# Gated linear attention: the product of keys and values in three rounded parts

## The chip, the cores and the metric

The kernel runs on one core of one Trainium2 chip. The metric is the device time of one execution in microseconds (us), as the median of several runs. A core has five engines that run side by side, each with a queue worked off in order: TensorE (PE in the profile, its weight loads PEld), VectorE (DVE), ScalarE (ACT), GpSimd (POOL) and SyncE (SP), which here only issues DMA transfers. Matrix products write to the banks of PSUM, and the other operands live in SBUF.

## The reference

One layer of a decoder: a normalised input is projected into the operands of two groups of heads, differential softmax attention (8 heads) and gated linear attention (4 heads). Both results are normalised and gated, joined, and projected out. The sequence has 1024 positions. Of this the change touches the gated heads alone:

```python
def gla_chunked(q, k, v, log_a):
    """S_t = diag(exp(log_a_t)) S_{t-1} + k_t^T v_t ; o_t = q_t S_t (q scaled by dk^-0.5)."""
    ...
    attn = jnp.where(causal, jnp.einsum('bhnik,bhnjk->bhnij', q_dec, k_inv), 0.0)
    o_intra = jnp.einsum('bhnij,bhnjv->bhniv', attn, v)

    def step(state, xs):
        qd, kt, vc, dl = xs
        o = jnp.einsum('bhck,bhkv->bhcv', qd, state)
        state = state * dl[..., None] + jnp.einsum('bhck,bhcv->bhkv', kt, vc)
        return state, o
```

The state of a head is 128 x 256 float32. The second product in `step`, keys times values, is what is changed.

## The kernel before, in words

The program has three stages. The first normalises the input and multiplies it by the input weights, in blocks of a seven-product scheme (`order`, `step`, `go`); the second is the softmax attention together with half of the output projection; the third ends the output projection. The gated heads have no stage of their own: they are a generator, `gla(g)`, put into the list `fill`, and each step of the first stage, twelve products of 512 columns in a bank x, y or z, advances it to its next `yield` (steps of the value blocks advance it twice). So work of the gated heads stands between the steps of the projection. TensorE's instructions keep the order in which the program writes them (`mm` and `tr` pin it); the instructions of the other engines and the DMA issues are put in order by the planner of the framework, and then run in that order on each engine's queue.

A projection step needs weights split into a rounded high part and a low part: a cast `w` on ScalarE, then a subtraction on VectorE, made up to three steps ahead in a ring of five. A product of full precision is then three rounded (fp32r) products, high by high, low by high and high by low. The gated heads, before, multiply in full float32 instead.

`gla(g)` works through a head in two halves of 512 positions, four blocks of 128 each. A half goes like this, with the number of steps in between:

- `gla_loads` has brought keys and queries (`kq`), values (`gv`) and decayed queries (`gqd`) from DRAM. The tile of the gates (`gg`) is taken.
- One step later: `pa`, the four blocks of scores, copied to `a`, the first half of the tile `gan`, and masked there by GpSimd; `pk`, the four keys transposed, copied to `kn`, the second half of `gan`. SP issues the load of the gates.
- Three steps later (two in the last half of all): `kv`, keys times values of a block into half a bank, and `gu`, the state, updated from it on VectorE. A head needs seven updates, four in its first half and three in its second.
- Two steps later: `gpo`, the output of each block from `a` and the state, copied to `go`.
- One step later: the loads of the next half are asked for, and the squares are summed (`sqs`, `sq_hl`).
- Three steps later (two in the last half): `gms`, the sum over the head, and the norm: `r` on ScalarE, then on VectorE and ScalarE `go` scaled, multiplied by the gates, and split again. The high part is written over the gates in `gg`, the low part over `go`, and SP stores both to `mixe` in DRAM.
- One step later the next half begins.

All of these tiles live in the pool `kp`, where each tag has one buffer: `q0` holds `kq`, `k0` holds `gv`, `ks0` holds `go`, `ks1` holds `gg`, and `k1` holds `gan`, then `sqs` and `sq_hl`. Who takes a tag next has to wait until all work on the tile before, transfers too, is done; the framework adds these waits.

Of the kernel before, what the change touches and what calls it, by code (L numbers as in the profile page):

```python
# [8 lines left out]
F32 = mybir.dt.float32  # L9
F32R = mybir.dt.float32r  # L10
AF = mybir.ActivationFunctionType
ALU = mybir.AluOpType
PSUM = bass.MemoryType.PSUM

P = 128
# [16 lines left out]
def hymba_kernel(  # L32
# [21 lines left out]
    pe, sp = nc.tensor, nc.sync  # L54
# [20 lines left out]
    act, dve, pool = Queue(nc.scalar), Queue(nc.vector), Queue(nc.gpsimd)  # L75

    def fp(t):
        return t.bitcast(F32)

    def cols(half):  # L80
        return slice(half * 512, half * 512 + 512)
# [40 lines left out]
    gg_d = [tc.dram_tile([2, P, S], F32, name=f"gg{g}_d") for g in range(GLA_HEADS)]  # L122
# [14 lines left out]
    def take_bank(shape, name):  # L137
        i = free.pop(0)
        return bank(i, shape, name), i
# [3 lines left out]
    def mm(*a, **k):  # L143
        tc.keep_in_program_order(pe.matmul(*a, **k))  # L144

    def tr(dst, src):
        tc.keep_in_program_order(pe.transpose(dst, src, ident))  # L147
# [29 lines left out]
    kp = ctx.enter_context(tc.tile_pool(name="kp", bufs=1))  # L177
# [6 lines left out]
    def t_c(name, dt=F32):  # L184
        return t2k("c", 4, name, dt)
# [838 lines left out]
    def gla_loads(g, half):  # L1024

        if g < GLA_HEADS and (g, half) not in loaded:
            cs = cols(half)
            kq = kp.tile([P, 2, 512], F32, tag="q0", name="kq")
            v = kp.tile([P, 2, 4, P], F32, tag="k0", name="gv")
            if not spare:  # L1030
                spare.append(kp.tile([P, 2, 512], F32, tag="q1", name="gqd"))
            qd = spare[0][:, 0]
            sp.dma_start(kq[:, 0], gq_d[g][2, :, cs])
            sp.dma_start(kq[:, 1], gq_d[g][0, :, cs])
            for t in range(2):
                sp.dma_start(v[:, t], gv_d[g][t, :, half * 4 : half * 4 + 4, :])
            sp.dma_start(qd, gq_d[g][1, :, cs])
            loaded[g, half] = kq, v, qd
        return loaded.get((g, half))

    def gla(g):

        u = None
        for half in range(2):
            cs = cols(half)
            kq, v, qd = gla_loads(g, half)
            gates = kp.tile([P, 2, 512], F32, tag="ks1", name="gg")
            yield
            if not g and not half:
                yield  # L1050
                yield
            o = kp.tile([P, 2, 512], F32, tag="ks0", name="go")
            an = kp.tile([P, 2, 4, P], F32, tag="k1", name="gan")
            a, kn = an[:, 0], an[:, 1]
            pa, ib = take_bank([P, 4, P], "pa")
            for i in range(4):
                c = slice(i * P, i * P + P)
                mm(pa[:, i, :], kq[:, 0, c], kq[:, 1, c], start=True, stop=True)
            free.append(ib)
            act.copy(a, pa)  # L1060
            pool.affine_select(
                a, a, [[0, 4], [1, P]], ALU.is_ge, 0.0, base=0, channel_multiplier=-1
            )
            pk, ib = take_bank([P, 4, P], "pk")
            for i in range(4):
                tr(pk[:, i, :], kq[:, 0, i * P : i * P + P])
            free.append(ib)
            act.copy(kn, pk)
            for t in range(2):
                sp.dma_start(gates[:, t], gg_d[g][t, :, cs])  # L1070
            last = g == GLA_HEADS - 1 and half == 1
            for _ in range(2 if last else 3):
                yield
            us = [u]
            for m in range(2):
                kv, ib = take_bank([P, 2, 256], "kv")
                n = half * 4 + 2 * m
                for i in range(min(2, NT - 1 - n)):
                    mm(
                        kv[:, i].rearrange("p (t c) -> p t c", c=P), kn[:, 2 * m + i, :],  # L1080
                        v[:, :, 2 * m + i, :], start=True, stop=True,
                    )
                for i in range(min(2, NT - 1 - n)):
                    u1, u = u, ap.tile([P, 256], F32, tag="gu", name="gu", bufs=5)
                    if u1 is None:
                        dve.tensor_copy(u, kv[:, i])
                    else:
                        dve.scalar_tensor_tensor(
                            u, u1, dsteps[g][:, n + i : n + i + 1], kv[:, i], ALU.mult, ALU.add
                        )  # L1090
                    us.append(u)
                free.append(ib)
            yield
            yield
            for m in range(2):
                po, ib = take_bank([P, 2, 256], "gpo")
                for i in range(2):
                    c = slice((2 * m + i) * P, (2 * m + i + 1) * P)
                    for t in range(2):
                        oc = po[:, t, i * P : (i + 1) * P]  # L1100
                        mm(
                            oc, v[:, t, 2 * m + i, :], a[:, 2 * m + i, :],
                            start=True, stop=(us[2 * m + i] is None),
                        )
                        if us[2 * m + i] is not None:
                            u_t = us[2 * m + i][:, t * P : (t + 1) * P]
                            mm(oc, u_t, qd[:, c], start=False, stop=True)
                act.copy(o[:, :, m * 256 : m * 256 + 256], po)
                free.append(ib)
            yield  # L1110
            gla_loads(*((g, 1) if half == 0 else (g + 1, 0)))

            sqs = kp.tile([P, 2, 512], F32, tag="k1", name="sqs")
            for t in range(2):
                act.activation(sqs[:, t], o[:, t], AF.Square)
            sq = t_c("sq")
            dve.tensor_tensor(sq, sqs[:, 0], sqs[:, 1], ALU.add)
            act.copy(sqs[:64, 1], sq[64:])
            dve.tensor_tensor(sq[:64], sq[:64], sqs[:64, 1], ALU.add)
            hl = kp.tile([P, 2, 512], F32R, tag="k1", name="sq_hl")[:, 0]  # L1120
            act.copy(hl[:64], sq[:64])
            dve.tensor_tensor(hl[64:], sq[:64], fp(hl[:64]), ALU.subtract)
            for _ in range(2 if last else 3):
                yield
            ms, ib = take_bank([P, 512], "gms")
            mm(ms, ones, hl, start=True, stop=True)
            r = t_c("r")
            act.activation(r, ms, AF.Ln, bias=eps_t, scale=1.0 / 256)
            free.append(ib)
            act.activation(r, r, AF.Exp, scale=-0.5)  # L1130
            m_hi = gates.bitcast(F32R)
            for t in range(2):
                dve.scalar_tensor_tensor(
                    o[:, t], o[:, t], gla_g[:, t : t + 1], r, ALU.mult, ALU.mult
                )
                dve.tensor_tensor(o[:, t], o[:, t], gates[:, t], ALU.mult)
                act.copy(m_hi[:, t], o[:, t])
                m_lo = o[:, t].bitcast(F32R)
                dve.tensor_tensor(m_lo, o[:, t], fp(m_hi[:, t]), ALU.subtract)
                for i, src in enumerate((m_hi[:, t], m_lo)):  # L1140
                    sp.dma_start(
                        mixe[half * 4 : half * 4 + 4, i, :, 2 * g + t, :].rearrange("s p c -> p s c"),
                        fp(src).rearrange("p (s c) -> p s c", c=P),
                    )
            yield
# [25 lines left out]

    go(order.index((7, 3)) + 1 - made[0])
    fill.append(chain(*(gla(g) for g in range(GLA_HEADS))))
    go(len(order) - made[0] - LEAD)
    for _ in fill[0] if fill else ():
# [671 lines left out]
```

## Time and profile before

| | us |
|---|---|
| median of 3 runs | 960.36 (960.04 to 960.93) |
| the profiled execution, its time | 960.34 |
| the profiled execution, its span | 958.6 |
| TensorE busy | 948.2 |
| VectorE busy | 742.3 |
| ScalarE busy | 604.7 |
| the gated heads' products kv, first to last start | 241.5 to 497.8 |

The span runs from the first instruction to the end of the last; the execution's time adds what lies around it. Times in the profile's views count from the start of the span. A name such as kv<-gv,gan tells what an instruction writes and reads. The length of a matmul in the profile is that of the whole pipeline; matmuls overlap, so the time that one occupies TensorE is the distance from its start to the next one's start. Lines are often those of a helper (L66 records all of ScalarE's, VectorE's and GpSimd's calls, L144 all products, L147 all transposes), so tiles tell more than lines.

### The profile page before, as it was taken

How to read it: one execution, taken by the hardware profiler on the slowest of the kernel's cores; microseconds unless marked ns; L12 is line 12 of the kernel's file. 1: busy time of each engine (PE TensorE's matmuls, PEld its weight loads, DVE VectorE, ACT ScalarE, POOL GpSimd, SP SyncE). 2: the span in 40 equal slices, each digit the busy share in tenths (PEclk: the TensorE clock that was granted, in tenths of full speed). 3: DMA queues.
4: the chain of work that ended last, by engine and by line, in shares of the span. 5: the costliest groups of instructions: out<-in, count | busy, mean ns of one | idle time of the engine just before them, and what ended most of it. 6: DMA issues, size and time to landing. Idle time of an engine off the chain costs nothing.

```text
span 958.6 us, 14358 instructions
## 1 busy us (share of the span) xinstructions
PE 948.2 (99%) x4624; PEld 793.2 (83%) x4624; DVE 742.3 (77%) x1476; ACT 604.7 (63%) x1162; POOL 193.9 (20%) x263
## 2 busy tenths in 40 slices
PE   9999999999999999999999999999999999999997
PEld 7877788888888888888888888888888888888885
DVE  5998799996778787687767476588888888898464
ACT  7753355845777556577765444366677677787773
POOL 2001002222141112131100002122222222433321
PEclk9999999999999999999999999999999999999999
DMA  8546367487577897986755498996665679994776
GB/s 285 162 149 172 91 203 244 168 293 249 188 255 242 275 305 255 295 258 216 263 175 154 143 298 265 411 291 217 220 223 193 222 230 349 331 291 105 160 206 141
DMA packets 153258, 220.34 MB, mean 230 GB/s; under 512 B 15776, under 2 KB 85664, under 8 KB 153088
## 3 DMA queue, kind: packets, MB, share of 16 engines
q1 hardware_dynamic: 138736, 177.65, 57.8%
q0 software_dynamic: 14448, 41.79, 14.8%
q8 instruction: 36, 0.59, 0.3%
q14 instruction: 38, 0.31, 0.1%
HBM read 133.93 MB, written 88.60 MB: 232 GB/s over the span
## 4 chain that ended last, share of the span: by engine, by line
PE 96%; DVE 1%; ACT 1%; DMA 1%; issue 0%; POOL 0%; SPq 0%; DVEq 0%; ACTq 0%
PE x L144 23%; PE z L144 16%; PE y L144 16%; PE ypart L144 14%; PE sc L144 7%; PE po L144 5%; PE yps L144 4%; PE wtr L147 3%; PE gpo L144 3%; PE kv L144 1%; PE gkl_ps L144 1%; PE pa L144 1%; PE xT L147 1%; DMA x<-in_x_dram 1%; PE ms L144 0%; PE pk L147 0%
## 5 line engine op out<-in xcount | busy, mean ns | idle before, releaser
L66 ACT CAST w<-w_raw 128x512 fp32r<-128x512 f32 x138 | 85.1, 620 | 70.0 <-PE y L144 31.7
L66 ACT ACTIVATE p<-p,stt 128x896 f32<-128x896 f32 (+7 forms) x128 | 99.3, 777 | 30.8 <-DVE stt L66 29.9
L66 DVE TENSOR_TENSOR w<-w_raw,w 128x512 fp32r<-128x512 f32 x138 | 94.0, 684 | 31.5 <-ACT w L66 31.4
L66 ACT COPY s<-x 128x512 f32<-128x512 f32 x78 | 44.7, 584 | 65.1 <-PE x L144 64.9
L66 DVE CUSTOM_DVE_ANT_0 p<-sc,maskt 128x512 f32<-128x512 f32 (+3 forms) x128 | 74.2, 585 | 14.5 <-PE sc L144 13.2
L66 POOL TENSOR_SCALAR p<-p,stt,lam 128x1024 f32<-128x1024 f32 (+3 forms) x64 | 55.9, 874 | 143.9 <-DVE stt L66 143.8
L144 PE MATMUL z<-s_hi,w 128*128 128x512 f32 x320 | 80.1, 393 | 0.0
L144 PE MATMUL x<-s_hi,w 128*128 128x512 f32 x320 | 80.0, 392 | 0.0
L144 PE MATMUL y<-h_hi,w 128*128 128x512 f32 x320 | 80.0, 392 | 0.0
L144 PE MATMUL ypart<-wo_hi,m_hi 128*128 128x512 f32 x192 | 79.5, 414 | 0.1
L144 PE MATMUL ypart<-wo_hi,m_lo 128*128 128x512 f32 x192 | 75.5, 393 | 0.0
L144 PE MATMUL ypart<-wo_lo,m_hi 128*128 128x512 f32 x192 | 75.4, 393 | 0.0
L66 POOL DMA_DIRECT2D wo_d<-wo_hi x32 | 17.4, 543 | 270.4 <-ACT wo_hi L66 270.4
L144 PEld LDWEIGHTS z<-s_hi,w 128*128 128x128 f32 x320 | 59.8, 188 | 12.3
L144 PEld LDWEIGHTS x<-s_hi,w 128*128 128x128 f32 x320 | 59.7, 188 | 12.3
L144 PEld LDWEIGHTS y<-h_hi,w 128*128 128x128 f32 x320 | 59.7, 188 | 12.2
L144 PE MATMUL sc<-k,q 128*128 128x512 f32 (+1 forms) x192 | 68.9, 362 | 0.1
L144 PE MATMUL sc<-ks,q 128*128 128x512 f32 (+1 forms) x192 | 66.1, 347 | 0.0
L66 ACT CAST wt_hi<-wtr 128x512 fp32r<-128x512 f32 (+1 forms) x80 | 42.8, 534 | 29.0 <-PE wtr L147 28.3
L66 DVE TENSOR_TENSOR wt_lo<-wtr,wt_hi 128x512 fp32r<-128x512 f32 (+1 forms) x80 | 50.6, 633 | 9.9 <-ACT wt_hi L66 9.1
L66 DVE TENSOR_TENSOR w_raw<-w_raw 128x512 f32<-128x512 f32 x80 | 56.2, 703 | 1.4 <-DMA w_raw<-in_w_in_dram 0.4
L66 DVE TENSOR_TENSOR c<-z,s 128x512 f32<-128x512 f32 x48 | 32.8, 687 | 31.3 <-ACT s L66 19.3
(234 smaller groups left out, 2348.0 us busy)
## 6 DMA issues: line engine op xcount, KB each, us to landing
w_raw<-in_w_in_dram SPq DMA_DIRECT2D x40, 512.0 KB, 4.9
wo_d<-wo_hi POOLq DMA_DIRECT2D x32, 256.0 KB, 3.0
q<-q_d SPq DMA_DIRECT2D x32, 256.0 KB, 5.3
k<-k_d SPq DMA_DIRECT2D x32, 256.0 KB, 5.5
ks<-k_d SPq DMA_DIRECT2D x64, 128.0 KB, 6.2
wo_raw<-in_w_out_dram POOLq DMA_DIRECT2D x31, 256.0 KB, 5.0
v<-v_d SPq DMA_DIRECT2D x14, 512.0 KB, 7.7
wo_d<-gqd POOLq DMA_DIRECT2D x22, 256.0 KB, 4.1
```

What stands on the lines that cost most here:

```text
L66: ins = op(*a, **k)
L144: tc.keep_in_program_order(pe.matmul(*a, **k))
L147: tc.keep_in_program_order(pe.transpose(dst, src, ident))
```

## The change

Keys times values, `kv`, becomes three fp32r products of 256 columns for each block in place of one float32 product. For that the values are split into `v_hi` and `v_lo` at the start of the half, and the transposed keys into `k_hi` and `k_lo` out of the bank `pk`. The tiles are dealt out anew: `v_hi` takes tag `ks0` and `v_lo` tag `ks1` until kv is done, after which `go` and the gates take them; the load of the gates goes behind kv. `k_hi` and `k_lo` take `k1`, and the masked scores `a` are written over the queries in `kq`. The loaded values `gv` stay as they are for `gpo`.

```diff
             kq, v, qd = gla_loads(g, half)
-            gates = kp.tile([P, 2, 512], F32, tag="ks1", name="gg")
             yield
...
-            o = kp.tile([P, 2, 512], F32, tag="ks0", name="go")
-            an = kp.tile([P, 2, 4, P], F32, tag="k1", name="gan")
-            a, kn = an[:, 0], an[:, 1]
+            v_hi = kp.tile([P, 4, 2, P], F32R, tag="ks0", name="gv_hi")
+            v_lo = kp.tile([P, 4, 2, P], F32R, tag="ks1", name="gv_lo")
+            for t in range(2):
+                act.copy(v_hi[:, :, t, :], v[:, t])
+                dve.tensor_tensor(v_lo[:, :, t, :], v[:, t], fp(v_hi[:, :, t, :]), ALU.subtract)
+            k_hl = kp.tile([P, 2, 512], F32R, tag="k1", name="gk_hl")
+            k_hi, k_lo = k_hl[:, 0], k_hl[:, 1]
+            a = kq[:, 1].rearrange("p (t c) -> p t c", c=P)
...
+            act.copy(k_hi, pk.rearrange("p t c -> p (t c)"))
+            dve.tensor_tensor(k_lo, pk.rearrange("p t c -> p (t c)"), fp(k_hi), ALU.subtract)
             free.append(ib)
-            act.copy(kn, pk)
-            for t in range(2):
-                sp.dma_start(gates[:, t], gg_d[g][t, :, cs])
...
-                    mm(
-                        kv[:, i].rearrange("p (t c) -> p t c", c=P), kn[:, 2 * m + i, :],
-                        v[:, :, 2 * m + i, :], start=True, stop=True,
-                    )
+                    k2 = 2 * m + i
+                    c = slice(k2 * P, k2 * P + P)
+                    for j, (k_p, v_p) in enumerate(((k_hi, v_hi), (k_hi, v_lo), (k_lo, v_hi))):
+                        mm(
+                            kv[:, i], k_p[:, c], v_p[:, k2].rearrange("p t c -> p (t c)"),
+                            start=not j, stop=j == 2,
+                        )
...
+            o = kp.tile([P, 2, 512], F32, tag="ks0", name="go")
+            gates = kp.tile([P, 2, 512], F32, tag="ks1", name="gg")
+            for t in range(2):
+                sp.dma_start(gates[:, t], gg_d[g][t, :, cs])
             yield
             yield
```

## The prediction

> **What bounds the kernel now.** I read the page's busy line and chain first, then the windows of the stage that the diff touches.
>
> ```profile
> PE 948.2 (99%) x4624; PEld 793.2 (83%) x4624; DVE 742.3 (77%) x1476; ACT 604.7 (63%) x1162; POOL 193.9 (20%) x263
> PE 96%; DVE 1%; ACT 1%; DMA 1%; issue 0%; POOL 0%; SPq 0%; DVEq 0%; ACTq 0%
> 276.00:312.00 36.00, 36.00 (x182) 30.65 (x182) 28.16 (x46) 23.83 (x44) 8.52 (x13) 1.00 0.84 260
> 422.00:458.00 36.00, 36.00 (x183) 30.65 (x182) 28.46 (x46) 27.53 (x51) 6.44 (x10) 1.00 0.74 243
> ```
>
> The chain that ends last is TensorE, 96% of it. In the windows (columns: stretch, length, then busy time of PE, PEld, DVE, ACT, POOL, then clock, DMA share, GB/s) TensorE is busy for all 36.00 of 36.00 us in a turn of the gated heads, while VectorE has 7.8 us free and ScalarE 12.2 or 8.5 us. So TensorE time saved here comes off the end, one for one, and a wait of TensorE here is added to the end, one for one. Work on VectorE and ScalarE is free unless TensorE waits for it. The whole question is therefore: how much shorter are the products, and do their operands arrive when TensorE gets there?
>
> **The products.** The view of tile kv gives their count, and the timeline their spacing (start, length, engine):
>
> ```profile
> L144 PE MATMUL kv<-gv,gan x56: 377/379/380, 241.5 to 497.8; 128*128 128x256 f32 x56
> 241.24 1.71 PEld L144 LDWEIGHTS kv<-gv,gan 128*128 128x128 f32 x8
> 242.97 1.10 PEld L144 LDWEIGHTS z<-s_hi,w 128*128 128x128 f32 x5
> 660.80 0.40 PE L144 MATMUL po<-wt_hi,v 128*128 128x256 f32 x2
> 661.03 0.28 PE L144 MATMUL po<-wt_lo,v 128*128 128x256 f32 x1
> 661.15 0.34 PE L144 MATMUL po<-wt_hi,v 128*128 128x128 f32 x2
> L144 PEld LDWEIGHTS po<-wt_hi,v x192: 187/188/193, 638.8 to 907.5; 128*128 128x128 f32 x192
> ```
>
> Four heads with 7 updates are 28 products, recorded as 56 instructions, so a full float32 product is two passes. The 379 ns of one is its pipelined length; what it occupies is the step from start to start: eight from 241.24 to 242.97, (242.97 - 241.24) / 8 = 0.216 us, 0.432 a product. The new products are rounded ones with 256 moving columns and a weight load each. Just that form stands in the attention values: three between 660.80 and 661.15, 0.35 / 3 = 0.117 us each, although each weight load is recorded as 188 ns long. Three of them make 0.35 us. The saving is 28 x (0.432 - 0.35) = 2.3 us; I take 2.2, as the first one behind 512-column work may not be as tight. The bounds of the step are 0.108 us (half a float32 pass over the same columns), which would save 3.0, and 0.188 us (weight loads that can't overlap): 84 x 0.188 - 56 x 0.216 = 3.7 us slower. I take the value of the po rows, since they are the same form.
>
> [...]
>
> **When the operands are there.** This is where I expect the change to lose. The tiles decide it. Before, kv reads the values straight from their loaded tile k0 and the transposed keys from k1; neither waits for a store of the previous half. After, the split values v_hi and v_lo live in ks0 and ks1, one buffer each. In the previous half ks0 holds the normalised output go, whose low parts are stored to mixe, and ks1 holds the gates, overwritten with the high parts and stored too. v_hi can't be written until the last store of go has landed, nor v_lo until those of gg have. That such a store holds up the next user of its buffer is already seen before, because the gates load uses ks1 (who waited for whom, SP's queue; us in total, times, longest):
>
> ```profile
> SPq L1070 <- DMA mixe<-gg: 12.1, 5, 4.6
> 278.79 0.33 SPq L1070 DMA_DIRECT2D gg<-gg_d  x1
> ```
>
> There the load waits 12.1 us in five cases, at no cost, since the gates are needed much later. kv isn't needed later. Here is one turn, from the sum of squares gms, after which the norm can start, to the next kv:
>
> ```profile
> 262.67 0.40 PE L144 MATMUL gms<-sq_hl,ones 128*128 128x512 f32 x1
> 264.76 0.68 ACT L66 ACTIVATE r<-gms,eps_t 128x512 f32<-128x512 f32 x1
> 267.63 1.41 DVE L66 SCALAR_TENSOR_TENSOR go<-go,gla_g,r 128x512 f32<-128x512 f32 x2
> 274.37 0.69 DVE L66 TENSOR_TENSOR go<-go,gg 128x512 fp32r<-128x512 f32 x1
> 277.88 1.46 PE L144 MATMUL kv<-gv,gan 128*128 128x256 f32 x6
> DMA to landing us min/median/max: 2.7/5.0/8.8
> ```
>
> TensorE's order is written out, so the distance from gms to kv is fixed: 277.88 - 262.67 = 15.2 us. In that time the norm runs on ScalarE and VectorE until 275.06, and only then is the last store issued. The last row is from the view of tile go, whose only transfers are these stores: 5.0 us from issue to landing at the median, 2.7 and 8.8 at the ends. All seven last stores, with the kv that follows each:
>
> ```profile
> 275.08 0.86 SPq L1141 DMA_DIRECT2D mixe<-go  x1
> 309.27 0.47 SPq L1141 DMA_DIRECT2D mixe<-go  x1
> 314.31 1.89 PE L144 MATMUL kv<-gv,gan 128*128 128x256 f32 x8
> 348.96 0.50 SPq L1141 DMA_DIRECT2D mixe<-go  x1
> 350.73 1.46 PE L144 MATMUL kv<-gv,gan 128*128 128x256 f32 x6
> 385.05 0.53 SPq L1141 DMA_DIRECT2D mixe<-go  x1
> 387.17 1.89 PE L144 MATMUL kv<-gv,gan 128*128 128x256 f32 x8
> 421.35 2.86 SPq L1141 DMA_DIRECT2D mixe<-go  x1
> 423.88 1.46 PE L144 MATMUL kv<-gv,gan 128*128 128x256 f32 x6
> 457.24 0.41 SPq L1141 DMA_DIRECT2D mixe<-go  x1
> 460.32 1.89 PE L144 MATMUL kv<-gv,gan 128*128 128x256 f32 x8
> 491.08 0.61 SPq L1141 DMA_DIRECT2D mixe<-go  x1
> 496.74 1.46 PE L144 MATMUL kv<-gv,gan 128*128 128x256 f32 x6
> ```
>
> Behind the landing stand two v_hi copies on ScalarE and the second v_lo on VectorE, 2 x 0.59 + 0.69 us by the rows below, with handovers 2.0 us. So the operands are ready 7.0 us after each issue, and TensorE would wait 4.2, 2.0, 5.2, 4.9, 4.5, 3.9 and 1.3 us: 26 us together. The first half of all has no store ahead of it and waits for nothing.
>
> Two things move that sum. The kq loads stand on SP just ahead of the stores in this turn, 1.24 and 0.42 us of queue time; after the change kq holds the masked scores until gpo has read them, so its loads go behind gpo, out of the way. I take 0.5 us off each turn for it, 26 - 3.5 = 22.5, and put the term at 23. Its ends: if all seven turns were like the two shortest (the stores at 309.27 and 491.08, 2.0 and 1.3 us of wait), 7 x 1.65 = 12; with the slowest landing, 8.8 us, 26 + 27 = 53. Below zero it can't go, as TensorE has other work up to kv's turn.
>
> **The other edits.**
>
> ```profile
> L66 ACT COPY gan<-pk x8: 585/596/602, 233.5 to 488.8; 128x512 f32<-128x512 f32 x8
> L66 DVE TENSOR_TENSOR w<-w_raw,w 128x512 fp32r<-128x512 f32 x138 | 94.0, 684 | 31.5 <-ACT w L66 31.4
> L66 DVE TENSOR_TENSOR w_raw<-w_raw 128x512 f32<-128x512 f32 x80 | 56.2, 703 | 1.4 <-DMA w_raw<-in_w_in_dram 0.4
> 270.14 1.24 SPq L1033 DMA_DIRECT2D kq<-gq_d  x1
> 271.44 0.42 SPq L1034 DMA_DIRECT2D kq<-gq_d  x1
> ```
>
> - Added on ScalarE: 2 copies in each of 8 halves, 16 x 0.59 = 9.4 us; the key copy only changes its type. Added on VectorE: 3 subtractions in each, 24 x 0.69 = 16.6 us. That is 1.2 and 2.1 us a turn, against 8.5 and 7.5 us free: nothing, while the weights stay ahead. Without that cover it is up to 26 us.
> - v_hi waits in ScalarE's queue, and behind it stand the casts w and the copies s of finished sums; VectorE waits the same way at v_lo. While TensorE waits at kv for the same landing, this costs nothing more. What is left over is the catching up, a rival below.
> - The gates loads move behind kv and now wait on SP for TensorE; behind them stands a w_raw load. VectorE waited only 0.4 us in all for w_raw, so these loads are early: nothing. Were they late, each would add up to the wait at kv once more, a case of rival 3. The gates are read only after the next gms, and a turn is 36 us long, of which 15.2 lie between gms and kv: some 20 us for a load that SP issued at 278.79 before. Nothing.
> - kq loads behind gpo have six steps of TensorE's order until the next scores (pa); the 15.2 us from gms to kv hold five. Nothing; if that cover failed, each half would pay what is left of the load, up to 5 us.
> - k_lo and the later release of the pk bank: 0.69 us with three steps until kv. Nothing.
>
> **The sum.** The profiled execution took 960.34 us, with a span of 958.6; the median of the runs is 960.36, so the two agree. 960.3 - 2.2 + 23 = 981 us.
>
> **The rivals.**
>
> 1. *The stores land in time: faster, 958.1 us.* It needs the last store to land 2.0 us before kv, 13.2 us after gms. For it: the norm in this turn is stretched by waiting, as r starts 1.7 us after gms ends, and two of the seven stores are issued 5.0 and 5.7 us ahead of kv. Against it: even those would need landings of 3.0 and 3.7 us, and the median is 5.0. All seven have to be in time; one or two late ones eat the 2.2 us.
> 2. *Short waits: 961 to 970 us.* The norm or its stores come 2 us earlier when the kq loads are gone, and the waits sum to 3 to 12.
> 3. *Waits that cost more than themselves: around 995 us.* ScalarE catches up after each landing. A copy s must be done before the next product adds into its bank, one step later; three held-up instructions of 0.6 us, some 2 us in each of 7 turns, are 14 us. Or the clock falls. The windows of the kernel's end show that it can:
>
> ```profile
> 946.00:952.00 6.00, 5.77 (x26) 4.45 (x24) 3.28 (x8) 2.06 (x7) 0.00 (x0) 1.00 0.68 160
> 952.00:955.40 3.40, 0.00 (x0) 0.00 (x0) 2.64 (x7) 1.00 (x4) 0.00 (x0) 1.00 0.02 10
> 955.50:958.60 3.10, 0.00 (x0) 0.00 (x0) 0.00 (x0) 0.00 (x0) 0.00 (x0) 0.50 0.40 145
> ```
>
> TensorE's last matmul ends at 951.8, and by 955.5 the granted clock is 0.50. Five of the seven waits above exceed these 3.7 us. If each paid for half a clock over the next 5 us, that is 5 x 2.5 = 12.5 us, 994. [...]
> 4. *The products don't get shorter*, as priced above at 0.188 us: 3.7 us slower in place of 2.2 faster, 987 with the waits. The po rows leave it little room, and it lies inside the main case's range.
>
> **How the numbers follow.** A measurement of this kernel can tell about 0.2%, 1.9 us, from no change. Chances: the main case with waits of 12 to 34 us, 970 to 992, 0.62 (rival 4 within it); rival 3, 0.16; rival 2, 0.10; rival 1, 0.09; gain and waits cancelling within 0.2%, 0.03. Faster 0.09, same 0.03, slower 0.88. The main case's own range is 970 to 992; the range of 8 in 10 takes in most of rivals 2 and 3, 964 to 1002.
>
> **What would show it.** Right: kv rows of 256 columns at 0.117 us, 84 of them; TensorE's busy time falls below its window in each turn but the first, with seven idle stretches of 1 to 8 us ahead of kv, ended by v_hi or v_lo; ScalarE (v_hi) waiting for the DMA mixe<-go; the attention stage unchanged but shifted. Wrong: TensorE still full in these windows, or the go stores landing over 2 us ahead of kv; idle TensorE elsewhere than at kv; a clock under 1.00 in these windows would speak for rival 3.

## The result, and the profile after

The changed kernel takes 988.83 us at the median of five runs (988.01 to 991.34), against 960.93 us for the kernel before: ratio 1.030, 95% interval 1.0289 to 1.0312. It is 28 us slower. The profiled execution has a span of 986.6 us, 28.0 over the span of before.

From the page of the changed kernel, the busy line and the chain:

```profile
PE 957.5 (97%) x4652; PEld 799.0 (81%) x4652; DVE 757.4 (77%) x1500; ACT 613.3 (62%) x1178; POOL 187.6 (19%) x263
PE 82%; DVE 8%; DMA 5%; issue 3%; ACT 2%; SPq 0%; DVEq 0%; POOL 0%; ACTq 0%
PE x L144 18%; PE ypart L144 13%; PE y L144 12%; PE z L144 12%; PE sc L144 7%; PE po L144 5%; PE yps L144 4%; PE wtr L147 3%; PE gpo L144 3%; DMA mixe<-go 2%; DVE c L66 2%; DVE go L66 2%; PE kv L144 2%; DMA q_d<-c 1%; DVE w L66 1%
```

TensorE's share of the chain has fallen from 96% to 82%, and the transfer mixe<-go stands in it, which before had no part in it. PE is busy for 9 us *more*, although its products are shorter: busy time counts microseconds, not work, and some of them ran at half the clock.

The timeline of TensorE in the changed kernel, gms and the starts of kv (in brackets the idle time ahead of an instruction, and what ended it):

```profile
262.87 0.40 PE L144 MATMUL gms<-sq_hl,ones 128*128 128x512 f32 x1
282.14 0.40 PE L144 MATMUL kv<-gv_hi,gk_hl 128*128 128x256 f32 x1 [3.90 <-ACT gv_hi L66]
282.95 0.58 PE L144 MATMUL kv<-gv_lo,gk_hl 128*128 128x256 f32 x1 [0.41 <-DVE gv_lo L66]
305.24 0.40 PE L144 MATMUL gms<-sq_hl,ones 128*128 128x512 f32 x1
320.45 0.28 PE L144 MATMUL kv<-gv_hi,gk_hl 128*128 128x256 f32 x1
341.76 0.40 PE L144 MATMUL gms<-sq_hl,ones 128*128 128x512 f32 x1
362.40 0.58 PE L144 MATMUL kv<-gv_hi,gk_hl 128*128 128x256 f32 x1 [5.27 <-ACT gv_hi L66]
403.53 0.38 PE L144 MATMUL kv<-gv_hi,gk_hl 128*128 128x256 f32 x1 [1.89 <-ACT gv_hi L66]
445.48 0.38 PE L144 MATMUL kv<-gv_hi,gk_hl 128*128 128x256 f32 x1 [2.46 <-ACT gv_hi L66]
486.13 0.39 PE L144 MATMUL kv<-gv_hi,gk_hl 128*128 128x256 f32 x1 [1.98 <-ACT gv_hi L66]
524.60 0.28 PE L144 MATMUL kv<-gv_hi,gk_hl 128*128 128x256 f32 x1
543.30 0.47 PE L144 MATMUL gms<-sq_hl,ones 128*128 128x512 f32 x1 [0.25 <-DVE sq_hl L66]
```

Read it by turns. From the first gms to the next were 36.4 us before (262.67 to 299.11); now they are 305.24 - 262.87 = 42.4. The next turn, whose kv at 320.45 doesn't wait for v_hi, takes 36.5. From the first gms to the last it is 280.4 us, against 252.6 before (515.25 - 262.67): 27.8 us of the 28.0 lie in these seven turns. The attention stage adds nothing.

Who holds v_hi up is said by ScalarE's timeline and SP's, here for the longest wait:

```profile
354.45 0.62 ACT L66 CAST w<-w_raw 128x512 fp32r<-128x512 f32 x1 [1.61 <-PE y L144]
361.21 1.14 ACT L66 CAST gv_hi<-gv 128x512 fp32r<-128x512 f32 x2 [6.14 <-DMA mixe<-go]
355.33 0.62 SPq L1151 DMA_DIRECT2D mixe<-go  x1
```

The last store is issued at 355.33, lands some 5.8 us later, and v_hi starts at once. ScalarE stood still for 6.14 us, and kv starts 1.2 us after v_hi did. The windows around that wait and around the first one show the second cost (last columns: granted clock, DMA share, GB/s):

```profile
278.97:282.37 3.40, 0.23 (x1) 0.19 (x1) 2.11 (x4) 1.14 (x2) 0.00 (x0) 1.00 0.79 263
282.38:285.78 3.40, 2.99 (x12) 2.64 (x12) 2.33 (x5) 0.00 (x0) 0.00 (x0) 0.50 0.00 0
357.47:360.88 3.41, 0.00 (x0) 0.00 (x0) 0.19 (x1) 0.00 (x0) 0.00 (x0) 1.00 1.12 354
360.89:367.70 6.81, 5.08 (x16) 4.20 (x17) 5.73 (x11) 3.81 (x7) 1.62 (x3) 0.50 0.35 124
483.77:487.17 3.40, 1.00 (x5) 0.42 (x4) 2.10 (x5) 2.14 (x4) 0.00 (x0) 1.00 0.98 356
487.18:490.58 3.40, 3.40 (x15) 3.11 (x15) 2.49 (x5) 0.00 (x0) 0.00 (x0) 0.50 0.49 148
```

Behind each of the five waits the clock is 0.50, for 3.4 us four times and for 6.8 us once; a product of 512 columns then takes 0.427 us (x<-h_hi from 365.08) in place of 0.227 (y<-h_hi from 369.07) from start to start.

Counted from start to start on TensorE, less the normal step, the waits at kv are 4.65, 0.3, 6.0, 3.2, 3.2, 2.7 and 0 us (v_hi and v_lo together), 20.0 in sum. The products save 1.9 us in these turns. That leaves 27.8 - 20.0 + 1.9 = 9.7 us for the half clock. A count that does not go by what is left over agrees: the stretches of half clock are 4 x 3.41 + 6.83 = 20.5 us long, TensorE is busy for 18.3 us of them, and half of that, an estimated 9.1 us, is what the full clock would have saved.

### The profile page after: what moved, and what is told of

Read it like the earlier page. It is cut to its first block, busy times and chain, and to the rows that moved or that the text cites. A ratio compares the mean times of both kernels' runs of the same rounds, so it can differ in the third digit from the quotient of the medians.

```text
span 986.6 us, 14471 instructions
## 1 busy us (share of the span) xinstructions
PE 957.5 (97%) x4652; PEld 799.0 (81%) x4652; DVE 757.4 (77%) x1500; ACT 613.3 (62%) x1178; POOL 187.6 (19%) x263
## 4 chain that ended last, share of the span: by engine, by line
PE 82%; DVE 8%; DMA 5%; issue 3%; ACT 2%; SPq 0%; DVEq 0%; POOL 0%; ACTq 0%
PE x L144 18%; PE ypart L144 13%; PE y L144 12%; PE z L144 12%; PE sc L144 7%; PE po L144 5%; PE yps L144 4%; PE wtr L147 3%; PE gpo L144 3%; DMA mixe<-go 2%; DVE c L66 2%; DVE go L66 2%; PE kv L144 2%; DMA q_d<-c 1%; DVE w L66 1%
## 5 line engine op out<-in xcount | busy, mean ns | idle before, releaser
L144 PEld LDWEIGHTS x<-s_hi,w 128*128 128x128 f32 x320 | 60.6, 191 | 12.5
```

## The experiments

The ratios below are those to the kernel before, run beside each on the same chip; before was 961.06, 960.88 and 960.84 us in the three groups.

### The stores out of the way

```diff
-                        fp(src).rearrange("p (s c) -> p s c", c=P),
+                        qd.rearrange("p (s c) -> p s c", c=P),
```

> The changed kernel, but the four stores of a half to mixe send the decayed queries (tile gqd) in place of the split output, with the same bytes; so the output part of the gated heads is left out of the result, and the tiles ks0 and ks1 are free as soon as VectorE has written them last. Theory (TensorE waits at kv because v_hi and v_lo must wait for the landing of these stores, and the clock falls because of that wait): the waits and the half clock are both gone, 958 to 959 us, 2 us below the kernel before. Rival A (the added copies and subtractions hold up the queues of ScalarE and VectorE): 966 or more, TensorE still waiting somewhere in the turns. Rival B (the kq loads that now go behind gpo are what is late): unchanged, 985 to 990.

Measured: 964.97 us (963.67 to 966.17), ratio 1.0040 (1.0028 to 1.0052). Of the 28 us, 24 go with the waiting for these four stores alone; the splits, the tiles, the kq loads and the products are all still there. Rival B falls. But the theory's 958 to 959 is missed by 6 us, and the timeline says where:

```profile
279.47 0.38 PE L144 MATMUL kv<-gv_hi,gk_hl 128*128 128x256 f32 x1 [1.33 <-ACT gv_hi L66]
281.91 0.39 PE L144 MATMUL kv<-gv_lo,gk_hl 128*128 128x256 f32 x1 [2.06 <-DVE gv_lo L66]
277.56 0.68 DVE L66 TENSOR_TENSOR go<-go,gg 128x512 fp32r<-128x512 f32 x1
278.27 1.14 ACT L66 CAST gv_hi<-gv 128x512 fp32r<-128x512 f32 x2 [0.88 <-DVE go L66]
280.57 1.28 DVE L66 TENSOR_TENSOR gv_lo<-gv,gv_hi 128x512 fp32r<-128x512 f32 x2
```

In this half even the last write of go, at 277.56, is too late for a kv due at 278, and gv_lo then stands behind other subtractions in VectorE's queue until 280.57, though v_hi was done at 279.4. Behind this wait the products of kv lie 0.21 us apart (four between 282.67 and 283.52), and the mean granted clock of the run is 0.997 against 0.998 before. This one turn takes 41.7 us in place of 36.4; one later kv waits another 0.8 us for v_lo. So a part of rival A is true: the norm's chain without the landing is barely short enough, and in this turn it isn't. An obvious remedy was not tried: buffers of their own for v_hi and v_lo, which would spare them both the landing and the last write of go. Whether SBUF has room for them, and what it would bring, no run shows.

### The old product on the new tiles

```diff
-                    for j, (k_p, v_p) in enumerate(((k_hi, v_hi), (k_hi, v_lo), (k_lo, v_hi))):
-                        mm(
-                            kv[:, i], k_p[:, c], v_p[:, k2].rearrange("p t c -> p (t c)"),
-                            start=not j, stop=j == 2,
-                        )
+                    mm(
+                        kv[:, i].rearrange("p (t c) -> p t c", c=P), fp(k_hi)[:, c],
+                        v[:, :, k2, :], start=True, stop=True,
+                    )
```

> The changed kernel with all of its splits, tiles and loads, but kv is one float32 product a block again, of the rounded keys k_hi and the values as loaded; the low part of the keys is left out. Theory: TensorE needs neither v_hi nor v_lo, so nothing waits at kv and the clock holds: 960.4 to 962 us, though ScalarE still waits for the stores ahead of v_hi. Rival A (what costs is ScalarE and VectorE standing still at v_hi and v_lo, with casts and copies behind them): 970 to 990 us, with waits of TensorE spread over the steps.

Measured: 963.40 us (962.16 to 964.30), ratio 1.0025 (1.0016 to 1.0034). ScalarE and VectorE still stand still at v_hi and v_lo:

```profile
355.89 1.14 ACT L66 CAST gv_hi<-gv 128x512 fp32r<-128x512 f32 x2 [6.50 <-DMA w_raw<-in_w_in_dram]
362.07 0.49 PE L144 MATMUL gpo<-gqd,gu 128*128 128x128 f32 x2 [0.95 <-DVE gu L66]
411.80 0.47 PE L144 MATMUL gms<-sq_hl,ones 128*128 128x512 f32 x1 [1.22 <-DVE sq_hl L66]
```

The first row's releaser is the wait that came last by the record; the landing of mixe<-go at 355.8 fits the start at 355.89 as well, so I read it as that store. Either way ScalarE is idle for 6.50 us, and TensorE does not notice until something behind it is late, once at gpo and once at gms, 2.4 us in all with a third wait of 0.2. That prices the standing queue: 2.3 us, a little above the 0 to 1.6 expected. Almost all of the loss needs kv itself to wait.

### Filling the waits

```diff
+            n_dummy = {(0, 1): 14, (1, 1): 20, (2, 0): 9, (2, 1): 9, (3, 0): 8}.get((g, half), 0)
+            if n_dummy:
+                ps, ib = take_bank([P, 512], "dummy")
+                for i in range(n_dummy):
+                    mm(ps, ones, at(H["h11"][0], 0), start=(i == 0), stop=(i == n_dummy - 1))
+                free.append(ib)
```

> The changed kernel with idle products (128x512, into a bank of their own) written just ahead of kv in the five halves in which TensorE waits: 14, 20, 9, 9 and 8 of them, 3.2, 4.5, 2.0, 2.0 and 1.8 us, somewhat less than each wait. Theory (about 18 to 20 us of the 28 are waiting, the other 10 are half clock brought on by it): the waits stay as long in all, filled, the clock stays at 1.00, 978 to 981 us. Rival C (the clock costs nothing of its own, the waits are all 28 us): 988 to 990 us, or more by what the idle products add.

Measured: 980.47 us (980.15 to 981.75), ratio 1.0205 (1.0192 to 1.0218), so 8.4 us less than the changed kernel, with 60 idle products more. The granted clock of the profiled run is 0.998, against 0.987.

```profile
278.00:286.00 8.00, 6.90 (x34) 5.37 (x33) 5.12 (x9) 1.76 (x3) 0.00 (x0) 1.00 0.58 182
```

The stretch that held the first wait and the first half clock is now at 1.00 throughout. Rival C falls: the clock costs 8.4 us of its own, near the 9.7 and 9.1 counted above. What is left, 19.5 us, is the waiting less the shorter products: from start to start the delays at kv, filled or idle, sum to 20.9 us in this trace, and one gms waits 0.7.

### The products alone

```diff
-                    mm(
-                        kv[:, i].rearrange("p (t c) -> p t c", c=P), kn[:, 2 * m + i, :],
-                        v[:, :, 2 * m + i, :], start=True, stop=True,
-                    )
+                    for j, part in enumerate((0, 1, 0)):
+                        mm(
+                            kv[:, i], at(H["h11"][part], j)[:, i * P : i * P + P],
+                            at(H["h12"][0], j)[:, :256], start=not j, stop=j == 2,
+                        )
```

> The kernel before with kv as three rounded products of 256 columns a block, taken from blocks of the projection's input that lie ready (h11, h12) in place of keys and values, so the gated heads' state is left out of the result; no split, no new tile, no moved load. Theory (the products themselves are shorter, and all of the loss is waiting and the clock): 2.2 us below the kernel before, 0.23%, ratio 0.9977 (0.997 to 0.9985), step between kv starts 0.117 us. Rival E (the shape costs more than in the attention values, weight loads show): ratio 1.000 to 1.004.

Measured: 959.70 us (958.90 to 960.21), ratio 0.9985 (0.9977 to 0.9994). The weight loads of twelve of them, first and last, and the next:

```profile
242.20 0.19 PEld L144 LDWEIGHTS kv<-h_hi,h_lo 128*128 128x128 f32 x1
243.39 0.19 PEld L144 LDWEIGHTS kv<-h_hi 128*128 128x128 f32 x1
243.51 1.70 PEld L144 LDWEIGHTS z<-s_hi,w 128*128 128x128 f32 x8
```

Eleven steps in 243.51 - 242.20 are 0.119 us each, as forecast. In the trace the seven turns shrink from 252.6 to 250.8 us, 1.8 for 24 of the 28 products, 2.1 for all. The timed runs give 1.2 us between the medians, and the interval of the ratio reaches from 0.6 to 2.2 us; the ratio lies at the small end of the forecast, 0.997 to 0.9985. In the profiled run the first gms stands 0.45 us later than before, and what lies behind the last gms is 0.8 us longer (444.2 for 443.4); the cause stays open. So the gain is there, but in full size only the trace of these turns shows it. Rival E falls.

### More room between the norm and kv

Four versions leave the stores as they are and deal the steps of a half out anew so that seven, not five, lie between gms and the next kv, taken from kv to gpo and from gpo to gms. The first (the remarks behind # are not in the code):

```diff
-            for _ in range(2 if last else 3):      # pk to kv
+            for _ in range(3 if last else 4):
...
-            yield
-            yield                                  # kv to gpo
+            yield
...
-            for _ in range(2 if last else 3):      # squares to gms
+            for _ in range(2):
...
-            yield                                  # after the norm
+            for _ in range(1 if last else 2):
+                yield
```

> The changed kernel with the steps between the parts of a half dealt out anew, the same number in all: four steps (not three) from pk to kv, one (not two) from kv to gpo, two (not three) from sq_hl to gms, two (not one) after the norm. From gms to the next kv TensorE then has seven steps in place of five, some 5.5 us more than 15.2. Theory: the waits of 4.7, 0.2, 6.0, 3.2, 3.2, 2.7 and 0 us shrink to about 0.5 in one half, the saving of 2.2 us shows, 958 to 960 us, faster than the kernel before. Rival A: 966 or more. Rival D (with one step from kv to gpo the state comes too late, a wait of 1 us or more in each half): 966 to 970, with TensorE waiting at gpo.

Measured: 969.01 us (966.39 to 971.07), ratio 1.0081 (1.0065 to 1.0098). TensorE's waits at kv are gone but for 0.3 us, so 20 of the 28 us come back. The theory's 958 to 960 is missed, by two new waits:

```profile
279.40 1.14 ACT L66 CAST gv_hi<-gv 128x512 fp32r<-128x512 f32 x2 [4.03 <-DMA mixe<-go]
280.45 0.58 ACT L66 COPY s<-x 128x512 f32<-128x512 f32 x1
281.08 2.70 PE L144 MATMUL x<-s_hi,w 128*128 128x512 f32 x8 [2.12 <-ACT s L66]
414.13 0.50 PE L144 MATMUL gms<-sq_hl,ones 128*128 128x512 f32 x1 [2.68 <-DVE sq_hl L66]
```

First, v_hi stands at the head of ScalarE's queue for 4.03 us with the copy s behind it, and the next product adds into the bank that s has to read first. That is rival A's mechanism, invisible as long as kv waited for the same landing. Second, gms now comes a step sooner, before its squares sq_hl are ready, which is like rival D but at gms. Behind the first of these waits the clock is 0.50 for 3.4 us (row in the last section); the mean granted clock of the run is 0.994, against 0.998 before.

The second puts v_hi later in ScalarE's queue, and its control is the kernel before with the same steps:

```diff
-            v_hi = kp.tile([P, 4, 2, P], F32R, tag="ks0", name="gv_hi")
...
-            for _ in range(2 if last else 3):
+            for i in range(3 if last else 4):
                 yield
+                if i == (1 if last else 2):
+                    v_hi = kp.tile([P, 4, 2, P], F32R, tag="ks0", name="gv_hi")
...
+                        with tc.issue_after(act.latest):
+                            act.copy(v_hi[:, :, t, :], v[:, t])
...
             yield
-            yield
             for m in range(2):
...
-            yield
             gla_loads(*((g, 1) if half == 0 else (g + 1, 0)))
...
-            yield
+            for _ in range(1 if last else 2):
+                yield
```

So the squares come right behind gpo, three steps ahead of gms, two in the last half.

> The changed kernel with the steps dealt out anew (four from pk to kv, one from kv to gpo, the squares right behind gpo and three steps before gms, two after the norm; the same number in all, seven from gms to the next kv) and with the splits of the values written three steps behind pk, their copies on ScalarE behind the copies and casts of that step. Theory, with what more_room showed (v_hi stood at the head of ScalarE's queue for 4.0 us, and TensorE then waited for a copy s behind it): the operands are in time and nothing stands behind a waiting v_hi, 958 to 961 us, ratio 0.998 to 1.001. Rival D (the shorter way from gpo to gms, three steps for four, makes gms late by 1 to 3 us in some halves, as in more_room): 961 to 966, with TensorE waiting at gms. Rival A (the added work itself): 966 or more.

> The kernel before with its steps dealt out as in late_split, and nothing else changed: what the new spacing costs by itself. Theory: nothing, 960.4, ratio 0.999 to 1.001. Rival D: 961 to 965 with waits at gms or gpo, and then the distance of late_split to this run, not to the kernel before, is what the split products are worth: 2.2 us less.

Measured: 991.12 us (988.20 to 991.70), ratio 1.0309 (1.0295 to 1.0323), and for the control 968.95 us (968.10 to 969.82), ratio 1.0084 (1.0070 to 1.0098). Both theories failed. The control loses 8 us by the steps alone, which is rival D's mechanism and more than its range, most of it at the last gms, where I had left two steps from gpo in place of three: TensorE is idle there for 4.7 us, and the mean granted clock of the run is 0.996. late_split has that wait too, 5.6 us, and its v_hi now comes too late: in four halves it starts when kv is due or nearly so. What stands ahead of it in ScalarE's queue differs from half to half: casts w, of which some wait for TensorE (1.6 us at 358.38), and activations and copies that ScalarE works through without a pause right ahead of it (v_hi at 244.40 and 516.34). The expectation of room3_late below puts it all down to the cast w; the trace shows that as one part only. TensorE waits 4.3 us for v_hi and 4.7 us for v_lo at kv in all. It also waits 2.05 us for a copy s behind a v_hi that waits 3.96 us for a landing, and 2.7 us at another gms; the mean granted clock is 0.986. So an instruction can stand too early in a queue or too late.

The third and fourth mend the last half; the fourth places v_hi behind the newest copy s instead. The third against the second:

```diff
-            for _ in range(2 if last else 3):      # squares to gms
+            for _ in range(3):
```

The splits stand where the change has them in the third, and two steps behind pk, behind the newest s, in the fourth.

> The changed kernel with the steps dealt out as in late_split but in the last half too three steps from the squares to gms (there late_split and its control had two, and gms came 5.7 and 4.8 us late), and the splits written where the change has them. Seven steps from gms to the next kv. Theory: kv has its operands; what is left are a copy s behind a waiting v_hi in one half (2 us and 1.7 of half clock, as in more_room) and gms about 1 us late in all, less the 2.1 of the products: 961 to 965 us, ratio 1.001 to 1.005. If that one wait doesn't come, 958 to 961. Rival A (the added work itself costs): 966 or more.

> The same as room3, but the splits of the values are written two steps behind pk, their copies on ScalarE behind the newest copy s of a finished sum (late_split put them behind the newest cast w, which waits for its place in the ring, so v_hi came when kv was already due). Theory: nothing of TensorE's needs stands behind a waiting v_hi, and v_hi comes at least 3 us ahead of kv: 958 to 961 us, ratio 0.997 to 1.001. Rival (any later place on ScalarE makes v_hi or v_lo late for kv): 964 to 990, with TensorE waiting at kv for v_hi or v_lo.

> The kernel before with its steps dealt out as in room3: the control for both. Theory: the 5 us at the last gms of late_split_before are gone, 960 to 962 us, ratio 0.999 to 1.002. Otherwise the shorter way from gpo to gms costs by itself, and the two above are to be held against this run.

Measured: room3 968.14 us (966.15 to 970.72), ratio 1.0078 (1.0066 to 1.0090); room3_late 968.66 us (967.69 to 969.77), ratio 1.0080 (1.0067 to 1.0093); room3_before 962.86 us (961.96 to 964.54), ratio 1.0024 (1.0013 to 1.0034). In the profiled run of room3 TensorE waits 0.4 us at kv in all, 0.9 once for s, and 3.9 at gms, 3.1 of it here:

```profile
480.85 0.69 DVE L66 TENSOR_TENSOR c<-y,s 128x512 f32<-128x512 f32 x1 [2.81 <-DMA g_d<-c]
483.55 0.50 PE L144 MATMUL gms<-sq_hl,ones 128*128 128x512 f32 x1 [3.15 <-DVE sq_hl L66]
```

The squares for gms stand behind a subtraction that waits for another store (g_d<-c) to land. The control pays 0.8 us at the same gms, so three steps from gpo to gms are barely too few by themselves, and with the split work the wait is longer. All three theories are missed: room3 lies where its rival A put it, 966 or more; room3_late lies in its rival's range, with that rival's wait at one kv; the control is 0.9 us above its range. Against their control, room3 and room3_late are still over 5 us slower, so the expected 2 us of gain doesn't show in any version that makes the splits. Which of the added pieces costs these 5 us I did not take apart; the waits in the two traces are at gms and, in room3_late, once more at kv (2.0 us for v_hi), with a mean granted clock of 0.995 against 0.998 in room3. room3's profiled run, at 966.15 us, is the fastest of its six, so its waits stand for less than the median's loss. No version here beats the kernel before in a usable way: products_alone is faster only because it makes no operands.

## Why the prediction was right

The forecast of 981 us in 964 to 1002 holds the measured 988.8, and the mechanism is the one named: five of seven kv, and not the first half's, wait for v_hi, and v_hi for mixe<-go. That the time lies in the main case's own 970 to 992 is in part luck: with the waits as they came, 20.0 us, and nothing for the clock, that case would have given 978. By its steps:

- *Products.* 0.117 us a step and 2.2 us saved: 0.119 and 2.1 in the trace of products_alone. Right.
- *Waits at kv, 23 us.* Measured 20.0. By half, 4.2, 2.0, 5.2, 4.9, 4.5, 3.9 and 1.3 were worked out, and 4.65, 0.3, 6.0, 3.2, 3.2, 2.7 and 0 came. The two halves that were to wait least did not wait for v_hi at all. The term was a little too large because the stores land faster now: the view of tile go in the changed kernel gives

```profile
DMA to landing us min/median/max: 2.2/3.4/6.5
```

  where before it was 5.0 at the median. The prediction gave 0.5 us a turn for moving the kq loads out of their way; the median fell by 1.6, though no run shows that the kq loads alone did that. Here too there is luck: the seven last stores that count took 5.7 us on average before, not 5.0, and by their own landings the waits would have been put at some 31 us in place of 26; now these seven take 4.0 us. The step from the landing to v_lo at kv, put at 2.0 us, came out at 1.9.
- *The clock, nothing in the main sum.* This is the step that was mis-sized. It stood as half of rival 3, at 0.16 for the whole rival, because the only row that showed a fall, at the kernel's end, had 3.7 us of idle TensorE. The prediction reckoned with a fall only behind waits longer than that. It came behind all five waits, the last of them of 1.98 and 0.42 us of recorded idle time (486.13, and v_lo at 486.94). The price in the rival, 2.5 us each or 12.5 in all, was too high: keep_clock measures 8.4 us for five. No run shows its 5 us behind each wait; in the changed kernel the half clock lasted 3.4 us four times and 6.8 us once.
- *Added work on ScalarE and VectorE, nothing.* old_product shows 2.3 us, and free_stores shows one half in which v_lo's place in VectorE's queue costs 2 us more. Behind the longer waits this was hidden, as argued; it surfaced as soon as they were gone.
- *Gates and kq loads, nothing.* Right: TensorE waited for neither, and free_stores, which keeps their new places, loses 24 of the 28 us.

The sum of before, with these sizes and the clock as keep_clock prices it: 960.3 - 2.1 + 20.0 + 8.4 = 986.6, against 988.8 measured; the 2.2 us between stay open. With the 9.7 us it gives 987.9, but that term was itself what was left over in the trace.

## What to carry to other kernels

Before operands are split into new tiles, list for each tag who held it last and when that holder's last transfer lands, and hold this against the place of the first reader in the order of the bounding engine; two microseconds saved on TensorE were paid for here with the landing of a store that nobody had waited for. An engine queue standing at such a wait is free only as long as the bounding engine waits for the same thing, so taking the first wait away brings out the next (2.12 us behind the copy s in more_room). And a wait of TensorE may not be over when it ends: behind each of the five waits here the clock was halved for 3.4 us or more.

## What the runs showed of the hardware

In the changed kernel the clock was 0.50 in five stretches behind the waits at kv, four of 3.4 us and one of 6.8. In the 3.4 us ahead of each, TensorE was busy for 0.23, 0.00, 0.69, 0.59 and 1.00 us, the first, second and fifth by the rows above, the others by these:

```profile
401.85:405.25 3.40, 0.69 (x3) 0.50 (x4) 3.21 (x6) 2.00 (x4) 1.63 (x3) 1.00 0.87 232
442.81:446.21 3.40, 0.59 (x2) 0.19 (x1) 2.07 (x4) 1.92 (x4) 1.08 (x3) 1.00 0.64 229
```

In more_room it was busy for 1.29 us, in the stretch that holds the wait for s:

```profile
278.96:282.37 3.41, 1.29 (x6) 1.08 (x7) 2.08 (x4) 2.66 (x5) 0.00 (x0) 1.00 0.52 188
282.38:285.78 3.40, 3.40 (x11) 2.73 (x10) 1.88 (x3) 0.25 (x1) 0.00 (x0) 0.50 0.50 154
```

In room3 a wait of 3.15 us, which ends with gms at 483.55, left the clock at 1.00:

```profile
478.44:481.85 3.41, 1.96 (x9) 1.31 (x7) 1.00 (x2) 0.36 (x2) 0.43 (x1) 1.00 0.71 279
481.86:485.26 3.40, 1.71 (x7) 1.42 (x8) 2.69 (x5) 3.40 (x7) 0.00 (x0) 1.00 0.33 90
```

So the length of a wait alone doesn't tell whether the clock falls: behind the last one in the changed kernel, of 1.98 and 0.42 us, it fell, and behind this longer one it didn't. Nor does the work just ahead: the 3.40 us that end with the wait in room3 hold some 3.40 - 3.15 = 0.25 us of it, about the 0.23 us ahead of the first fall. What decides, no run here shows. (The ends of products are modelled, so recorded work is itself an approximation.)
